# Head norms of memory queries and band queries taken as the scale of the softmax exponential

## The chip, the cores and the metric

The kernel runs on one core of one Trainium2 chip. Its time is the device time of one execution in microseconds (us); three runs of the kernel before gave 1013.49, 1013.75 and 1013.94 us, so the median is 1013.75 us. The engines go by the names of the profile: PE is TensorE (matrix multiply), PEld its weight load, DVE is VectorE, ACT is ScalarE, POOL is GpSimd and SP is the engine that starts the weight transfers. PSUM is the memory of eight banks into which TensorE writes; a bank holds 512 floats per partition.

## The reference

A decoder trunk of two layers on 256 tokens of width 1024, with a memory of 256 tokens. Each layer is an FFN, a mixer and an FFN. Layer 0 mixes with an mLSTM (mixer A below), layer 1 with sliding-window attention of 16 heads of width 64 (mixer B). Both mixers also hold four memory heads of width 128. Queries of the memory heads and of the band heads are normalised per head before their scores are formed:

```python
def rms_norm(x, g):
    y = xf * lax.rsqrt(jnp.mean(xf * xf, axis=-1, keepdims=True) + EPS)
    return y * g

# memory heads
q = rms_norm(xq.reshape(bsz, t, M_HEADS, M_HD), q_norm_g)
s = jnp.einsum('bthd,bmhd->bhtm', q, k) * M_HD ** -0.5
p = jax.nn.softmax(s, axis=-1)
# band heads
q = apply_partial_rope(rms_norm(q, q_norm_g), cos, sin) * B_HD ** -0.5
s = jnp.where(valid, jnp.einsum('bqhgd,bkhd->bhgqk', qn, kn), -jnp.inf)
m = jnp.maximum(jnp.max(s, axis=-1, keepdims=True), sink)
p = jnp.exp(s - m)
denom = jnp.sum(p, axis=-1, keepdims=True) + jnp.exp(sink - m)
```

The norm is one number per token and head. Rotation turns pairs of columns of a row and the scores are linear in the row, so this number may be applied to the row or, later, to the scores.

## The kernel before

Weights are read from memory in tiles of 128 x 1024 and split into a high part (ScalarE, line 213, `wh`) and a low part (VectorE, line 214, `wl`), and each projection product is made of three matmuls (lines 227 to 229, `mm3`). Projections are made in groups of 256 columns: one group fills one PSUM bank with 16 triples, which is 48 matmuls, and the code yields after every four triples, which is 12 matmuls.

The order of TensorE and of SP is the order in which the program emits. Around the main line of groups a class `Weave` keeps a clock of its own, `wv.now`, which each emitted matmul advances by a fixed amount (0.328 for a triple, 0.107 for a transpose, and so on). Side chains are spawned with a delay from the table `LAT`; at each yield of the main line the chains whose time has come are emitted. The order on VectorE, ScalarE and GpSimd is made by the scheduler of the compiler from its own cost model, and each engine then works strictly in that order.

A memory group (two heads, `cross_spawn`, line 595) goes like this. Its bank of raw rows is normalised by `head_norm` (line 395): a square on ScalarE, a sum per head on VectorE (L401), a scale and EPS on VectorE (L404), the power -1/2 on GpSimd (L406), a scale on VectorE (L408), and a multiply of the whole bank into an SBUF tile (L410), after which the bank is free. After a delay `cross` TensorE transposes that tile (L238), ScalarE copies the result out with the gain (`gqk`), and after `cross_s` and `cross_m` the two heads' scores are formed (L233, `bank<-kT,u`). Each head then takes the negated row maximum on VectorE (L618) and the exponential on ScalarE with that maximum as its bias, normalises (L622, L623), transposes the weights, copies them out (L630) and multiplies by the values (L233, `bank<-t,vM`).

A band group (256 columns, four heads of one kind, in mixer B at the end of the file) is normalised in the same way, rotated by `rope` (L884 to L887) in the SBUF tile, and after a delay `query` transposed and copied out with the gain (`gcut`). Each of its two chunks then runs `head`: mask matmuls (L947) and scores (L952) into two banks, four row maxima (L956, L957), the minimum with the sink (L959) and its difference (L960), four exponentials with the maximum as bias, a sum and reciprocal (L968, L969), four multiplies (L973), transposes (L238), copies (L981) and the product with the values (L988).

In mixer B the order of the groups is: keys and values together with the first memory group, the second memory group, four band groups, then the output projection, which keeps four of the eight PSUM banks for itself. In mixer A the two memory groups are followed by the groups of the mLSTM. The keys of the memory and of the band also go through `head_norm`.

Of the kernel before, what the change touches and what calls it, by code (L numbers as in the profile page):

```python
# [32 lines left out]
def constants():  # L33
# [16 lines left out]

LAT = dict(pieces=1, norm=8.5, mnorm=3.5, x0=17.0, mkeys=7.2, cross=9.5, cross_s=1.5,
           cross_m=3.7, cross_p=8.7, cross_o=3.0, gates=20.0, scores=2.2, scores_m=8.4, num=6.9, num_r=7.5,
           keys=5.5, keys_d=7.2, query=9.0, head=1.5, head_m=2.5, head_p=9.3, head_o=4.0)


WARM = 18
# [40 lines left out]
def tile_trunk(ctx: ExitStack, tc: tile.TileContext, a, out):  # L99
# [292 lines left out]
        nc.vector.tensor_scalar_mul(c[:, 2:4], rc, hd ** -0.5 if scaled else 1.0)  # L392
        return c

    def head_norm(dst, src, n, hsc):

        hd = src.shape[2] // n
        sq, v, u = tmp(), col(), col()
        sqv = sq[:, :, :n * hd]
        act(sqv, src, AF.Square)  # L400
        nc.vector.tensor_reduce(out=v[:, 0:2 * n].rearrange("p (h m) -> p h m", h=2),  # L401
                                in_=sqv.rearrange("p h (m d) -> p h m d", m=n), axis=AX.X, op=ALU.add)
        for h in range(2):
            nc.vector.tensor_scalar(u[:, n * h:n * h + n], v[:, n * h:n * h + n], hsc[:, h:h + 1], EPS,  # L404
                                    op0=ALU.mult, op1=ALU.add)
        nc.gpsimd.tensor_tensor(out=u[:, 8:8 + 2 * n], in0=u[:, 0:2 * n], in1=mhalf[:, 0:2 * n], op=ALU.pow)  # L406
        for h in range(2):
            nc.vector.tensor_scalar(v[:, 8 + n * h:8 + n * h + n], u[:, 8 + n * h:8 + n * h + n],  # L408
                                    hsc[:, 2 + h:3 + h], None, op0=ALU.mult)
        tt(out=dst.rearrange("p h (m d) -> p h m d", m=n), in0=src.rearrange("p h (m d) -> p h m d", m=n),  # L410
           in1=v[:, 8:8 + 2 * n].rearrange("p (h m) -> p h m", h=2).unsqueeze(3).to_broadcast([P, 2, n, hd]),
           op=ALU.mult)

    def turn(rows):
# [179 lines left out]

    def cross_spawn(gr, gi, layer, hsc, ys):
        qn = unit(F32)
        head_norm(qn, gr.ps, 2, hsc)
        cell = []

        def queries():  # L600
# [9 lines left out]
        def head(m):  # L610
            hd, qT = gi * 2 + m, cell[0]
            hi, lo = ys.tiles(4 + gi)
            s = mo()
            for h in range(2):
                mmf(s[:, h * T:(h + 1) * T], qT[:, m, h * P:(h + 1) * P], kT[gi][:, m], T)
            sv = halves(s)
            c = col()
            nc.vector.tensor_reduce(out=c[:, 2:4], in_=sv, axis=AX.X, op=ALU.max, negate=True)  # L618
            p = unit(F32)
            for h in range(2):  # L620
                act(p[:, h], sv[:, h], AF.Exp, bias=c[:, 2 + h:3 + h], accum_out=c[:, 4 + h:5 + h])
            nc.vector.reciprocal(c[:, 6:8], c[:, 4:6])  # L622
            tt(out=p, in0=p, in1=c[:, 6:8].unsqueeze(2).to_broadcast([P, 2, T]), op=ALU.mult)  # L623
            yield LAT['cross_p']
            tps = mo()
            for mc in range(2):
                for h in range(2):
                    transpose(tps[:, mc * T + h * P:mc * T + (h + 1) * P], p[:, h, mc * P:(mc + 1) * P])
            pT = tmp()
            nc.scalar.copy(pT, halves(tps))  # L630
# [259 lines left out]
    def mixer_b(x, nxt):  # L890
# [34 lines left out]
        def v22(x4):  # L925
            return x4.rearrange("p (h e) -> p h e", h=2)

        def queries(gi, qn):
            ps = turn(qn)
            qr = unit(F32)  # L930
            act(qr, ps, AF.Copy, scale=gcut[:, 0:1])
            for m in range(2):
                wv.spawn(head(2 * gi + m, qr), LAT['head'] + LAT['head_m'] * m)
            return
            yield

        def head(ch, qr):
# [17 lines left out]
            for e, s in enumerate(sc):  # L955
                nc.vector.tensor_reduce(out=c[:, e:e + 1], in_=s[:, :P], axis=AX.X, op=ALU.max, negate=True)  # L956
                nc.vector.tensor_reduce(out=c[:, 2 + e:3 + e], in_=s[:, P:384], axis=AX.X, op=ALU.max, negate=True)  # L957
            snk = nsink[:, 2 * ch:2 * ch + 2].unsqueeze(1).to_broadcast([P, 2, 2])
            tt(out=v22(c[:, 8:12]), in0=v22(c[:, 0:4]), in1=snk, op=ALU.min)  # L959
# [94 lines left out]
```

## Time and profile before

| | |
|---|---|
| median of three runs | 1013.75 us (1013.49 to 1013.94) |
| profiled execution | span 1011.9 us from the first to the last instruction; its time outside the span is not listed |
| mean granted TensorE clock | 0.997 |
| busy PE, DVE, ACT, POOL | 996.4, 673.3, 524.0, 28.5 us |

The profile page gives busy times, the chain of work that ended last, and groups of instructions by line. A row of a group reads: line, engine, operation, destination<-source, shape, count, then busy us, mean ns of one, and idle us of the engine before them with what ended it. A row of the timeline reads: start and duration in us, engine, line, operation, count, and in brackets the idle time before it with its releaser. A wait row reads: engine, operand and line that waited, what released it, then us in total, times, longest. A row of a window reads: start and end, length, then busy time and count for PE, PEld, DVE, ACT and POOL, the granted TensorE clock, the DMA share and GB/s. Names ending in q are an engine's instruction queue. Line 134 is a helper through which all activations of ScalarE go, and lines 227 to 229 and 233 are helpers for matmuls.

### The profile page before, as it was taken

The page shows a single profiled execution, that of the slowest core. Times are in us where ns is not written, and L with a number is a line of the kernel's source. Part 1 is how long each engine was busy: PE and PEld are TensorE (multiplying, and loading weights), DVE is VectorE, ACT ScalarE, POOL GpSimd, SP SyncE. Part 2 cuts the span into 40 slices and gives each one's busy share as a digit, 9 for nine tenths or more (in the row PEclk, how much of TensorE's full clock was granted, in tenths as well). Part 3 has the DMA queues.
Part 4 walks back from the last instruction along what each step waited for, and adds up shares of the span by engine and source line. Part 5 has one row for each costly group of instructions (what it writes and reads, how often), then busy time and mean ns, then how long its engine had stood idle before and what let it go on. Part 6 is the DMA issues. An engine that isn't in the chain of part 4 may idle for free.

```text
span 1011.9 us, 20587 instructions
## 1 busy us (share of the span) xinstructions
PE 996.4 (98%) x8560; PEld 978.2 (97%) x8560; DVE 673.3 (67%) x1116; ACT 524.0 (52%) x771; POOL 28.5 (3%) x27
## 2 busy tenths in 40 slices
PE   8899999999999999999999999999999999999998
PEld 7899999999999999999999999999987899999998
DVE  6876665668756786666568666656787768666551
ACT  7755444456566564454445444544557665454440
POOL 1100000000100000000000000000121000000000
PEclk9999999999999999999999999999999999999999
DMA  9676666667644566665666666566632247665650
GB/s 310 209 247 189 193 190 180 190 187 204 184 131 138 178 191 199 193 191 178 192 206 201 200 189 192 178 194 199 189 115 81 87 137 222 199 190 183 189 171 22
DMA packets 173205, 182.71 MB, mean 181 GB/s; under 512 B 7124, under 2 KB 168328, under 8 KB 173112
## 3 DMA queue, kind: packets, MB, share of 16 engines
q1 hardware_dynamic: 171872, 179.60, 58.3%
q10 hardware_dynamic: 1016, 1.58, 0.5%
q8 instruction: 67, 1.10, 0.5%
q0 software_dynamic: 224, 0.22, 0.2%
q14 instruction: 26, 0.21, 0.1%
HBM read 180.32 MB, written 1.05 MB: 179 GB/s over the span
## 4 chain that ended last, share of the span: by engine, by line
PE 92%; DVE 4%; ACT 1%; POOL 1%; DMA 1%; issue 0%; SPq 0%; POOLq 0%; ACTq 0%; DVEq 0%
PE bank L227 29%; PE bank L228 29%; PE bank L229 29%; PE bank L233 2%; DVE wl L214 1%; PE bank L238 1%; POOL col L406 1%; ACT u L134 1%; DMA wr<-in_mem_w_kv_dram 1%; PE bank L988 1%; DVE col L401 0%; DVE u L410 0%; DVE u L973 0%; DVE col L957 0%; ACT wh L213 0%
## 5 line engine op out<-in xcount | busy, mean ns | idle before, releaser
L214 DVE TENSOR_TENSOR wl<-wr,wh 128x1024 fp32r<-128x1024 f32 (+1 forms) x347 | 414.7, 1196 | 267.0 <-ACT wh L213 266.2
L213 ACT CAST wh<-wr 128x1024 fp32r<-128x1024 f32 (+1 forms) x347 | 356.9, 1031 | 391.8 <-PE bank L228 367.4
L227 PE MATMUL bank<-xh,wh 128*128 128x256 f32 x1544 | 427.8, 277 | 0.0
L228 PE MATMUL bank<-xl,wh 128*128 128x256 f32 x1544 | 426.4, 276 | 0.0
L229 PE MATMUL bank<-xh,wl 128*128 128x256 f32 x1544 | 426.4, 276 | 0.0
L227 PEld LDWEIGHTS bank<-xh,wh 128*128 128x128 f32 x1544 | 290.0, 188 | 0.1
L228 PEld LDWEIGHTS bank<-xl,wh 128*128 128x128 f32 x1544 | 289.8, 188 | 0.1
L229 PEld LDWEIGHTS bank<-xh,wl 128*128 128x128 f32 x1544 | 289.8, 188 | 0.0
L227 PE MATMUL bank<-u,wh 128*128 128x256 f32 x896 | 249.3, 278 | 0.0
L228 PE MATMUL bank<-u,wh 128*128 128x256 f32 x896 | 247.6, 276 | 0.0
L229 PE MATMUL bank<-u,wl 128*128 128x256 f32 x896 | 247.6, 276 | 0.0
L227 PEld LDWEIGHTS bank<-u,wh 128*128 128x128 f32 x896 | 168.2, 188 | 1.9 <-issue 1.7
L228 PEld LDWEIGHTS bank<-u,wh 128*128 128x128 f32 x896 | 168.3, 188 | 0.1
L229 PEld LDWEIGHTS bank<-u,wl 128*128 128x128 f32 x896 | 168.3, 188 | 0.0
L227 PE MATMUL bank<-wh,xh 128*128 128x256 f32 x208 | 60.3, 290 | 0.0
L228 PE MATMUL bank<-wl,xh 128*128 128x256 f32 x208 | 58.7, 282 | 0.0
L229 PE MATMUL bank<-wh,xl 128*128 128x256 f32 x208 | 58.5, 281 | 0.0
L503 DVE TENSOR_TENSOR t<-bank,rb 128x256 f32<-128x256 f32 x88 | 36.3, 420 | 6.7 <-PE bank L229 6.7
L227 PEld LDWEIGHTS bank<-wh,xh 128*128 128x128 f32 x208 | 39.8, 191 | 0.5 <-issue 0.3
L228 PEld LDWEIGHTS bank<-wl,xh 128*128 128x128 f32 x208 | 39.8, 191 | 0.1
L229 PEld LDWEIGHTS bank<-wh,xl 128*128 128x128 f32 x208 | 39.8, 191 | 0.0
L506 DVE TENSOR_TENSOR t<-t,bank 128x256 f32<-128x256 f32 x88 | 32.7, 413 | 0.0
(182 smaller groups left out, 671.0 us busy)
## 6 DMA issues: line engine op xcount, KB each, us to landing
wr<-in_ffn_w_in_dram SPq DMA_DIRECT2D x176, 512.0 KB, 4.3
wr<-in_ffn_w_out_dram SPq DMA_DIRECT2D x80, 512.0 KB, 3.7
wr<-in_a_w_in_dram SPq DMA_DIRECT2D x28, 512.0 KB, 3.7
wr<-in_b_w_in_dram SPq DMA_DIRECT2D x14, 512.0 KB, 4.6
wr<-in_a_w_out_dram SPq DMA_DIRECT2D x12, 512.0 KB, 3.4
wr<-in_b_w_out_dram SPq DMA_DIRECT2D x12, 512.0 KB, 3.4
wr<-in_ffn_w_out_dram SPq DMA_DIRECT2D x16, 256.0 KB, 2.9
wr<-in_mem_w_kv_dram SPq DMA_DIRECT2D x7, 512.0 KB, 7.8
```

Source lines behind the costliest of these rows:

```text
L134: ins = nc.scalar.activation(*args, **kw)
L213: last[0] = nc.scalar.copy(hi[:, i * n:(i + 1) * n], src[:, i * n:(i + 1) * n])
L214: tt(out=lo[:, i * n:(i + 1) * n], in0=src[:, i * n:(i + 1) * n], in1=hi[:, i * n:(i + 1) * n].bitcast(F32), op=ALU.subtract)
L227: nc.tensor.matmul(ps, wh, xh, start=start, stop=False, skip_group_check=True)
L228: nc.tensor.matmul(ps, wh, xl, start=False, stop=False, skip_group_check=True)
L229: nc.tensor.matmul(ps, wl, xh, start=False, stop=stop, skip_group_check=True)
L233: nc.tensor.matmul(ps, lhsT, rhs, start=start, stop=stop, skip_group_check=True)
L238: nc.tensor.transpose(ps, src, ident[:k, :k])
L406: nc.gpsimd.tensor_tensor(out=u[:, 8:8 + 2 * n], in0=u[:, 0:2 * n], in1=mhalf[:, 0:2 * n], op=ALU.pow)
L503: tt(out=t[:, m], in0=ps[m][:, :T], in1=x.rb, op=ALU.mult)
L506: tt(out=t[:, m], in0=t[:, m], in1=ps[m][:, T:], op=ALU.mult)
L988: nc.tensor.matmul(o[es[e], cs], vr[:, i, js], pTs[e][:, src], start=i == 0, stop=i == 1, skip_group_check=True)
```

## The change

`head_norm` is cut in two. The new `head_factor` makes only the factor per row and head and returns it; `head_norm` calls it and multiplies, and still serves the keys. For memory groups and band groups the bank is now copied raw by ScalarE into the SBUF tile, and the factor is made beside it. Transposes, rotation and scores take the raw rows. In each head the negated maximum of the raw scores is multiplied by the factor on VectorE, and the exponential takes the factor as its scale per partition. Two delays of the emitting clock are changed: `cross` from 9.5 to 5.0 and `query` from 9.0 to 6.5.

```diff
-LAT = dict(... cross=9.5, ... query=9.0, ...)
+LAT = dict(... cross=5.0, ... query=6.5, ...)
...
-    def head_norm(dst, src, n, hsc):
+    def head_factor(src, n, hsc):
         hd = src.shape[2] // n
         sq, v, u = tmp(), col(), col()
...
         for h in range(2):
             nc.vector.tensor_scalar(v[:, 8 + n * h:8 + n * h + n], u[:, 8 + n * h:8 + n * h + n],
                                     hsc[:, 2 + h:3 + h], None, op0=ALU.mult)
+        return v[:, 8:8 + 2 * n].rearrange("p (h m) -> p h m", h=2)
+
+    def head_norm(dst, src, n, hsc):
+        f = head_factor(src, n, hsc)
+        hd = src.shape[2] // n
         tt(out=dst.rearrange("p h (m d) -> p h m d", m=n), in0=src.rearrange("p h (m d) -> p h m d", m=n),
-           in1=v[:, 8:8 + 2 * n].rearrange("p (h m) -> p h m", h=2).unsqueeze(3).to_broadcast([P, 2, n, hd]),
+           in1=f.unsqueeze(3).to_broadcast([P, 2, n, hd]),
            op=ALU.mult)
...
     def cross_spawn(gr, gi, layer, hsc, ys):
         qn = unit(F32)
-        head_norm(qn, gr.ps, 2, hsc)
+        nc.scalar.copy(qn, gr.ps)
+        f = head_factor(gr.ps, 2, hsc)
...
-            nc.vector.tensor_reduce(out=c[:, 2:4], in_=sv, axis=AX.X, op=ALU.max, negate=True)
+            nc.vector.tensor_reduce(out=c[:, 0:2], in_=sv, axis=AX.X, op=ALU.max, negate=True)
+            tt(out=c[:, 2:4], in0=c[:, 0:2], in1=f[:, :, m], op=ALU.mult)
             p = unit(F32)
             for h in range(2):
-                act(p[:, h], sv[:, h], AF.Exp, bias=c[:, 2 + h:3 + h], accum_out=c[:, 4 + h:5 + h])
+                act(p[:, h], sv[:, h], AF.Exp, scale=f[:, h, m:m + 1], bias=c[:, 2 + h:3 + h],
+                    accum_out=c[:, 4 + h:5 + h])
...
         def head(ch, qr, f):
...
+            tt(out=v22(c[:, 0:4]), in0=v22(c[:, 0:4]), in1=f, op=ALU.mult)
             snk = nsink[:, 2 * ch:2 * ch + 2].unsqueeze(1).to_broadcast([P, 2, 2])
...
-                    act(p[e][:, cs], sc[e][:, cs], AF.Exp, bias=c[:, 8 + i:9 + i],
+                    act(p[e][:, cs], sc[e][:, cs], AF.Exp, scale=f[:, h, e:e + 1], bias=c[:, 8 + i:9 + i],
                         accum_out=d[:, 4 + i:5 + i])
...
             qn = unit(F32)
-            head_norm(qn, gr.ps, 4, hsq)
+            nc.scalar.copy(qn, gr.ps)
+            f = head_factor(gr.ps, 4, hsq)
             rope(qn, 4, 0)
-            wv.spawn(queries(gi, qn), LAT['query'])
+            wv.spawn(queries(gi, qn, f), LAT['query'])
```

More of the change, by code (lines that the diff above doesn't have):

```diff
@@ L49 @@
 G_MEM, G_F1, G_MIX, G_F2, G_XQ, G_XK, G_AH, G_BQ, G_BK, G_END = 0, 8, 24, 40, 56, 58, 60, 68, 69, 70
-LAT = dict(pieces=1, norm=8.5, mnorm=3.5, x0=17.0, mkeys=7.2, cross=9.5, cross_s=1.5,
+LAT = dict(pieces=1, norm=8.5, mnorm=3.5, x0=17.0, mkeys=7.2, cross=5.0, cross_s=1.5,
            cross_m=3.7, cross_p=8.7, cross_o=3.0, gates=20.0, scores=2.2, scores_m=8.4, num=6.9, num_r=7.5,
-           keys=5.5, keys_d=7.2, query=9.0, head=1.5, head_m=2.5, head_p=9.3, head_o=4.0)
+           keys=5.5, keys_d=7.2, query=6.5, head=1.5, head_m=2.5, head_p=9.3, head_o=4.0)
 WARM = 18
@@ L926, in v22, with queries @@
             return x4.rearrange("p (h e) -> p h e", h=2)
-        def queries(gi, qn):
+        def queries(gi, qn, f):
             ps = turn(qn)
@@ L932, in queries, with head @@
             for m in range(2):
-                wv.spawn(head(2 * gi + m, qr), LAT['head'] + LAT['head_m'] * m)
+                wv.spawn(head(2 * gi + m, qr, f[:, :, 2 * m:2 * m + 2]), LAT['head'] + LAT['head_m'] * m)
             return
             yield
-        def head(ch, qr):
+        def head(ch, qr, f):
             while wv.now < st.get("at", 1e9):
```

## The prediction

> **What bounds the kernel now.** I read the page first, for the span, the busy times and the chain that ended last.
>
> ```profile
> span 1011.9 us, 20587 instructions
> ...
> PE 996.4 (98%) x8560; PEld 978.2 (97%) x8560; DVE 673.3 (67%) x1116; ACT 524.0 (52%) x771; POOL 28.5 (3%) x27
> ...
> PE 92%; DVE 4%; ACT 1%; POOL 1%; DMA 1%; issue 0%; SPq 0%; POOLq 0%; ACTq 0%; DVEq 0%
> ```
>
> TensorE sets the time. The change removes and adds no matmul, so it can move the end only through the time in which TensorE stands still or runs slowly. The span is 1.85 us below the median of 1013.75 us; I sum changes of the span and apply them to the median. Next I asked for busy times by stage. 230 to 363 us holds the memory-matrix mixer, mixer A; 720 to 838 us holds the band mixer, mixer B. Columns: window, length, PE, PEld, DVE, ACT, POOL, clock.
>
> ```profile
> 230.00:363.00 133.00, 133.00 (x1104) 131.00 (x1103) 98.70 (x213) 79.89 (x140) 7.05 (x6) 1.00 0.54 164
> ...
> 720.00:838.00 118.00, 113.29 (x918) 102.37 (x917) 88.31 (x240) 73.19 (x178) 13.60 (x8) 0.99 0.38 117
> ```
>
> In mixer A TensorE is never idle. Only mixer B has something to win: 118.00 - 113.29 = 4.71 us of idle and a clock of 0.99. The waits of TensorE (engine, line, releaser: us, times, longest) name nearly all of it, 4.64 us:
>
> ```profile
> PE bank L233 <- ACT u L134: 2.4, 1, 2.4
> ...
> PE bank L952 <- ACT u L134: 0.9, 1, 0.9
> PE bank L947 <- DVE u L410: 0.8, 1, 0.8
> PE bank L988 <- ACT u L134: 0.4, 1, 0.4
> ...
> PE bank L947 <- ACT t L981: 0.2, 1, 0.2
> ```
>
> The timeline shows how the first comes about:
>
> ```profile
> 737.42 1.03 PE L233 MATMUL bank<-kT,u 128*128 128x256 f32 x4
> ...
> 739.65 0.60 PE L238 MATMUL bank<-con,u 128*128 128x128 f32 x4
> ...
> 739.76 2.48 POOL L406 TENSOR_TENSOR col<-col,mhalf 128x8 f32<-128x8 f32 x1 [3.46 <-DVE col L404]
> ...
> 742.25 0.28 PE L229 MATMUL bank<-wh,xl 128*128 128x256 f32 x1
> ...
> 742.27 0.36 DVE L408 TENSOR_SCALAR col<-col,qsc 128x4 f32<-128x4 f32 x2 [1.53 <-POOL col L406]
> ...
> 742.54 0.69 DVE L618 TENSOR_REDUCE col<-bank 128x2 f32<-128x512 f32 x1
> ...
> 743.26 0.47 ACT L134 ACTIVATE u<-bank,col 128x256 f32<-128x256 f32 x1 [5.46 <-DVE col L618]
> ...
> 744.17 0.69 ACT L134 ACTIVATE u<-bank,gqk 128x512 f32<-128x512 f32 x1
> ...
> 744.91 1.13 PE L233 MATMUL bank<-kT,u 128*128 128x256 f32 x4 [2.38 <-ACT u L134]
> ```
>
> The first memory scores ran at 737.42. Their maximum (L618) is queued on VectorE behind L408, the head norm of band group 0, which waits for the power on GpSimd. The exponential on ScalarE waits 5.46 us for that maximum, and behind it stands the copy (gqk) of the second memory group's transposes, which TensorE had made at 739.65. TensorE waits 2.38 us for that copy. Then the clock falls (window, length, PE; the clock is the number after POOL), and the same happens after the large waits at the start:
>
> ```profile
> 745.90:749.40 3.50, 3.50 (x18) 3.50 (x17) 2.98 (x7) 2.60 (x10) 0.00 (x0) 0.51 0.37 101
> ...
> 26.50:32.50 6.00, 1.92 (x14) 1.51 (x13) 4.48 (x16) 4.65 (x7) 2.06 (x2) 1.00 0.00 2
> 32.50:36.00 3.50, 3.50 (x19) 3.50 (x18) 3.33 (x6) 1.71 (x3) 1.22 (x1) 0.51 0.57 165
> ```
>
> Its price: the same 24 projection matmuls take 750.25 - 745.69 = 4.56 us there and 737.42 - 734.51 = 2.91 us at full clock, so 1.65 us.
>
> ```profile
> 734.51 0.36 PE L227 MATMUL bank<-wh,xh 128*128 128x256 f32 x1
> ...
> 745.69 0.51 PE L227 MATMUL bank<-wh,xh 128*128 128x256 f32 x1
> ...
> 750.25 0.27 PE L238 MATMUL bank<-con,u 128*128 128x128 f32 x1
> ```
>
> In all, mixer B loses 4.64 + 1.65 = 6.29 us. The change can gain no more than that.
>
> **The change part by part.** *Removed:* the multiply L410 for two memory groups in A and six query groups in B. *Added:* one ScalarE copy per group, one small VectorE multiply per head (4 memory heads per mixer, 8 band chunks), and a scale read per partition in every exponential. Prices from groups of mixer B:
>
> ```profile
> L410 DVE TENSOR_TENSOR u<-bank,col 128x512 f32<-128x512 f32 x6 | 4.1, 690 | 0.3
> ...
> L630 ACT COPY t<-bank 128x512 f32<-128x512 f32 x4 | 2.4, 604 | 0.9 <-PE bank L238 0.9
> ...
> L134 ACT ACTIVATE u<-bank,gqk 128x512 f32<-128x512 f32 x2 | 1.4, 688 | 0.8 <-PE bank L238 0.8
> ...
> L959 DVE TENSOR_TENSOR col<-col,nsink 128x4 f32<-128x4 f32 x8 | 1.3, 160 | 0.2
> ...
> L134 ACT ACTIVATE u<-bank,col 128x256 f32<-128x256 f32 x24 | 11.5, 479 | 7.8 <-DVE col L618 7.8
> ...
> L134 ACT ACTIVATE u<-bank,col 128x128 f32<-128x128 f32 x16 | 6.0, 376 | 9.7 <-DVE col L959 9.7
> ```
>
> VectorE in B: minus 4.1, plus 12 x 0.160 = 1.9, net -2.2 of 88.3 us. ScalarE in B: six copies of 0.604 = 3.6; the scale costs 688 - 604 = 84 ns on a full tile, and on 24 + 16 exponentials 3.4 us; 73.2 becomes 80.2 of 118 us. In A: -1.4 + 0.6 us on VectorE, +1.2 + 0.7 us on ScalarE. Both engines stay under TensorE, so this load costs nothing as a sum. It counts only where TensorE waits for a chain: a band head's exponentials become 4 x 0.084 + 0.16 = 0.5 us longer, a memory head's 0.33 us. The bound from below is 0 (hidden), from above about 0.5 us at each place where TensorE already waits for such a chain.
>
> *Moved:* the raw rows need no sum of squares, no power and no L408. The delays fall to 5.0 (memory queries) and 6.5 (band queries). TensorE's order follows a host clock whose increments stand in the code (0.328 per three projection matmuls, 0.107 per transpose), so both orders can be written down by hand; the one of before agrees with the trace. Call X0, X1 the memory groups, Q0 to Q3 the band groups, H their heads, "4" a quarter of a group (12 matmuls). Before: X1 whole, Q0 4, key turn, Q0 8, X0 turn, Q0 4, Q1 4, X0.0 scores, Q1 4, X1 turn, X0.1 scores, Q1 4, X1.0 scores. After: X1 whole, X0 turn, key turn, Q0 4, X0.0 scores, Q0 8, X0.1 scores, X1 turn, Q0 4, Q1 4, X1.0 scores. No DMA and no weight load changes place, so SP's order stays; GpSimd keeps its powers.
>
> Is the work ready in time? X0's turn comes 12 matmuls before the place of the old key turn (730.89); at 2.91 / 24 = 0.12 us each that is 729.4, where it was 734.15. Its raw copy comes at the latest behind the value copies, in the place of the square at 727.81, and so ends by 728.4. The keys' rows end at 729.94, for a turn at 729.8 (four transposes take 734.51 - 734.15 = 0.36 us) in place of 730.89: 0 to 0.2 us of new wait, I take 0.1. X0.0's scores follow at 731.6; the copy of X0's turn starts behind at most one raw copy and ends near 731.1.
>
> ```profile
> 727.81 0.60 ACT L134 ACTIVATE t<-bank 128x512 f32<-128x512 f32 x1
> ...
> 729.46 0.48 DVE L916 COPY u<-t 128x256 f32<-128x256 f32 x2
> ...
> 730.89 0.60 PE L238 MATMUL bank<-con,u 128*128 128x128 f32 x4
> ...
> 734.15 0.60 PE L238 MATMUL bank<-con,u 128*128 128x128 f32 x4
> ```
>
> The new wait is that of the exponentials for the factor, through the multiply of the maximum. X0's factor existed before the old turn at 734.15, at the latest at 733.5 (a multiply of 0.69 stood between); its exponential then starts by 734.3, and behind it on ScalarE stand weight casts and the copy of X1's turn, which TensorE wants only two thirds of a group later. Q0's factor has the time from its group's end, near 738, to H0's scores, some ten microseconds.
>
> X0.0's maximum is due near 732.4, long before Q0's power starts (Q0 ends near 738), and 24 matmuls stand between X1's turn and X1.0's scores in place of 12 and a memory score. The place of the 2.38 us wait is dissolved: I take the full 2.38 and, with no long gap, the 1.65 of the clock.
>
> The Trainium skill, "TensorE: Matmul & The Clock Gate", section "HAM oscillation — how this bites in real kernels", lets the clock fall only after gaps of more than about 3.4 us. By that rule a 2.4 us gap would not explain the slow window and its 1.65 us need not return (estimate by it: a gain of 3.1 us before losses). The trace shows the fall right behind a single wait of 2.38 us, and once more behind a stretch with 4.1 of 6 us idle, so I go by the trace.
>
> The 0.8 us wait at L947 is for the bank of Q3, held until L410:
>
> ```profile
> 783.67 0.69 DVE L410 TENSOR_TENSOR u<-bank,col 128x512 f32<-128x512 f32 x1
> ...
> 784.42 0.32 PE L947 MATMUL bank<-maskb,identb 128*128 128x384 bf16 x1 [0.75 <-DVE u L410]
> ```
>
> After the change the bank comes free when copy and square (2 x 0.6 us) are done, without sums and power: gain 0.75.
>
> The 0.9 us wait is that of the band scores for the copy of Q1's turn, which stood behind the exponentials of two heads:
>
> ```profile
> 758.98 0.60 PE L238 MATMUL bank<-con,u 128*128 128x128 f32 x4
> ...
> 759.12 0.37 ACT L134 ACTIVATE u<-bank,col 128x128 f32<-128x128 f32 x1 [1.53 <-DVE col L959]
> ...
> 762.74 0.74 ACT L134 ACTIVATE u<-bank,gcut 128x512 f32<-128x512 f32 x1
> ```
>
> The scores were due 0.9 us before that copy's end at 763.5, 3.6 us after the turn. By the host clock the distance from Q1's turn to H2's scores falls from 3.4 to 2.7, or some 2.9 us; but H1's exponentials now lie further ahead of the turn. Bounds: -0.9 (the wait goes) and +1.4 (the copy as late as now, 4.5 us, and 8 x 0.084 later, against 2.9, less the 0.9 that stands). I take 0, the wait as it is, near the middle. In the output projection four banks are bound to it, and H6, H7 and the transposes of H5 now follow each other closer: a bank wait there, bounded by 0 and the time for which a head's four exponentials hold it (2 x 0.479 + 2 x 0.376 and the scale, some 2 us); I take 0.5, nearest to the 0.2 and 0.4 that stand there now.
>
> In mixer A X0's turn moves behind the whole of X1's group, which is 5.8 us of matmuls against a copy of 0.6 us; I cost it at 0, and what hides the added work there is that cover.
>
> Sum: -2.38 - 1.65 - 0.75 + 0.1 + 0.5 = -4.2 us; 1013.75 - 4.2 = 1009.6 us.
>
> **The rivals.** (1) *All waits go:* the band-score and bank waits vanish too: -6.29, 1007.5 us. For it: less VectorE work, banks free earlier. Against it: ScalarE gets 7 us more. Chance 0.14. (2) *The clock does not come back:* the half-speed window had another cause than the wait and falls anyway: -4.2 + 1.65, 1011.2 us. For it: 2.38 us is less than the window's own 3.5. Against it: both windows stand behind idle stretches. Chance 0.09. (It is what the rule of the Trainium skill's "TensorE: Matmul & The Clock Gate", cited above, would give.) (3) *The stall moves to the band queries:* the copy of Q1's turn stays behind two heads' exponentials (759.12 to 762.74), with a cover of only 2.9 us: a wait of 0.9 + 1.4 = 2.3 us, enough for a slow window again, 1.4 + 1.65 = 3.1 us back; 1012.7 us. Chance 0.12. (4) *Slower:* the same mechanism at Q1 and at Q2, whose distance shrinks by the host clock from 3.4 to 2.7 as well: 3.1 + 2.3 + 1.65 = 7.1 us back, 1016.7 us. It decides once two such copies end over 2.3 us late; one alone isn't enough. For it: VectorE's and ScalarE's order is planned by a model that already misplaced L408. Against it: the heads before Q2 are spread wider. Chance 0.15. That the scores come no earlier because the raw copy is itself late is within (3).
>
> **How the numbers follow.** My forecast has 0.50. A measurement of this kernel tells about 0.2% (2 us) from no change. Faster: the forecast, (1), (2) and a small part of (3), 0.74; same: the rest of (3), 0.11; slower: (4), 0.15. The range reaches from a little below all waits gone, 1007.0, past (3) to 1014.0, and leaves out (4) and little else. The likeliest case alone: 1008.5 to 1010.8.
>
> **What would show it.** Right: no wait of over 1 us at L233 behind ScalarE; clock 1.00 through 720 to 838; X0's turn near 729.4; no wait of the mask matmuls (L947 now) for a query group's bank; mixer A still without idle TensorE. Wrong: a wait of over 2.4 us at the band scores with a half-clock window behind it, or mixer B's idle again over 4 us; idle TensorE in mixer A.

## The result and the profile after

The changed kernel takes 1025.71 us (1024.69 to 1028.57, 4 runs) against 1013.85 us (1013.49 to 1014.39) for the kernel before: a ratio of 1.0115, with a 95% interval of 1.0103 to 1.0127. It is slower by 1.15%, where I had forecast 1009.6 us and a range up to 1014.0. The profiled run took 1026.1 us.

The page of the changed kernel: span, busy time of the engines, share of each engine in the chain that ended last.

```profile
span 1024.3 us, 20611 instructions
...
PE 1000.6 (98%) x8560; PEld 980.7 (96%) x8560; DVE 670.7 (65%) x1124; ACT 532.1 (52%) x779; POOL 24.5 (2%) x27
...
PE 88%; DVE 5%; ACT 3%; POOL 1%; issue 1%; DMA 1%; SPq 0%; ACTq 0%; POOLq 0%
```

The load moved as worked out: VectorE 2.6 us less, ScalarE 8.1 us more, the same 8560 matmuls. But in the chain VectorE has 5% instead of 4 and ScalarE 3% instead of 1. The span grew by 12.4 us. I measure each mixer from the matmul of its own norm (L308) to the next norm's: mixer A went from 133.05 to 137.07 us, mixer B from 115.53 to 124.12, together 12.6 us; the rest of the program gives back 0.2.

Windows of the changed kernel over mixer A, mixer B and three short stretches (columns as in the prediction; the number after POOL is the granted clock):

```profile
229.40:366.50 137.10, 134.59 (x1105) 132.41 (x1104) 98.41 (x214) 81.54 (x142) 6.32 (x6) 0.99 0.52 160
725.90:850.10 124.20, 114.01 (x897) 101.60 (x897) 84.98 (x244) 78.28 (x182) 10.27 (x8) 0.97 0.34 107
270.60:274.00 3.40, 3.40 (x17) 3.40 (x16) 1.77 (x3) 1.79 (x5) 0.00 (x0) 0.50 0.30 66
772.30:775.70 3.40, 3.40 (x17) 2.80 (x14) 2.95 (x10) 1.23 (x3) 0.00 (x0) 0.50 0.02 5
789.40:792.80 3.40, 3.32 (x16) 2.67 (x17) 2.45 (x11) 1.59 (x5) 1.20 (x1) 0.50 0.14 45
```

Mixer A, never idle before, now has 2.51 us of idle TensorE and a stretch at half clock. Mixer B has 10.2 us of idle instead of 4.7, and two stretches at half clock instead of one. With 1.65 us for each such stretch (the price worked out in the prediction) that is 2.5 + 1.65 in A and 5.5 + 1.65 in B, 11.3 of the 12.6 us. Another 1.4 us of mixer B is longer busy time of TensorE that I did not trace to one place.

The waits of TensorE in the changed kernel (line, releaser: us in total, times, longest):

```profile
PE bank L233 <- ACT u L134: 4.2, 2, 2.5
PE bank L961 <- ACT u L134: 3.9, 3, 2.7
...
PE bank L956 <- ACT u L134: 2.0, 3, 1.1
```

These are scores and masks that wait for ScalarE's copy of a turn (the transposed queries) or for a bank that exponentials hold. The chain behind the first of them, in mixer A (timeline: start, duration, engine and line; in brackets how long the engine had waited and for whom):

```profile
258.64 1.02 PE L233 MATMUL bank<-kT,u 128*128 128x256 f32 x4
...
260.32 1.01 POOL L406 TENSOR_TENSOR col<-col,mhalf 128x4 f32<-128x4 f32 x1 [1.46 <-DVE col L404]
261.36 0.36 DVE L408 TENSOR_SCALAR col<-col,qsc 128x2 f32<-128x2 f32 x2 [1.12 <-POOL col L406]
261.63 0.69 DVE L625 TENSOR_REDUCE col<-bank 128x2 f32<-128x512 f32 x1
262.23 1.22 DVE L214 TENSOR_TENSOR wl<-wr,wh 128x1024 fp32r<-128x1024 f32 x1
262.33 1.03 PE L233 MATMUL bank<-kT,u 128*128 128x256 f32 x4
...
263.20 0.60 PE L238 MATMUL bank<-con,u 128*128 128x128 f32 x4
263.36 0.15 DVE L626 TENSOR_TENSOR col<-col,col 128x2 f32<-128x2 f32 x1
...
264.84 0.17 DVE L631 RECIPROCAL col<-col 128x2 f32<-128x2 f32 x1 [1.33 <-ACT u L134]
...
265.65 0.68 DVE L625 TENSOR_REDUCE col<-bank 128x2 f32<-128x512 f32 x1
266.25 1.22 DVE L214 TENSOR_TENSOR wl<-wr,wh 128x1024 fp32r<-128x1024 f32 x1
...
267.38 0.15 DVE L626 TENSOR_TENSOR col<-col,col 128x2 f32<-128x2 f32 x1
...
267.63 0.56 ACT L134 ACTIVATE u<-bank,col,col 128x256 f32<-128x256 f32 x1 [1.88 <-DVE col L626]
...
268.73 0.68 ACT L134 ACTIVATE u<-bank,gqk 128x512 f32<-128x512 f32 x1
...
269.47 1.13 PE L233 MATMUL bank<-kT,u 128*128 128x256 f32 x4 [2.51 <-ACT u L134]
```

X0.0's scores end at 259.66, but their maximum (L625) starts only at 261.63. VectorE runs its instructions in order, and ahead of the maximum stands L408 of the *other* group's factor, which waits for the power on GpSimd. Then comes the second delay: between each maximum (L625) and its multiply (L626) stands a weight cast (L214, 1.22 us), so that the exponential, which needs the multiply's result, starts over a microsecond later. The delay of the first head is passed on to the second: X0.1's scores end at 263.36, but its maximum starts 2.29 us later, because the normalisation of X0.0 (L631) stands ahead of it and waits for X0.0's late exponentials. The copy of X1's turn (gqk) stands behind X0.1's exponentials on ScalarE; TensorE had made that turn at 263.20 and waits 2.51 us for the copy.

The memory place of mixer B is the one whose wait I had called dissolved. Timeline:

```profile
735.55 1.03 PE L233 MATMUL bank<-kT,u 128*128 128x256 f32 x4
...
736.84 1.22 DVE L214 TENSOR_TENSOR wl<-wr,wh 128x1024 fp32r<-128x1024 f32 x1
737.98 0.67 DVE L401 TENSOR_REDUCE col<-t 128x4 f32<-128x512 f32 x1
...
738.95 0.69 DVE L625 TENSOR_REDUCE col<-bank 128x2 f32<-128x512 f32 x1
...
740.23 0.36 DVE L408 TENSOR_SCALAR col<-col,qsc 128x2 f32<-128x2 f32 x2 [0.59 <-POOL col L406]
740.50 0.15 DVE L626 TENSOR_TENSOR col<-col,col 128x2 f32<-128x2 f32 x1
...
745.27 1.13 PE L233 MATMUL bank<-kT,u 128*128 128x256 f32 x4 [1.74 <-ACT u L134]
```

The scores end at 736.58; a weight cast and the other group's sum of squares (L401) put the maximum off by 2.4 us, and L408 puts the multiply off once more. At the band queries the same two things come together, with the longest wait of all:

```profile
760.34 0.93 PE L961 MATMUL bank<-u,u 64*128 64x128 f32 x8
...
765.35 0.36 DVE L408 TENSOR_SCALAR col<-col,qsc 128x4 f32<-128x4 f32 x2 [1.55 <-POOL col L406]
...
766.05 0.63 PE L238 MATMUL bank<-con,u 128*128 128x128 f32 x4 [0.76 <-DVE u L896]
766.16 0.28 DVE L965 TENSOR_REDUCE col<-bank 128x1 f32<-128x128 f32 x1
...
767.55 0.15 DVE L967 TENSOR_TENSOR col<-col,col 128x4 f32<-128x4 f32 x1
767.62 1.21 DVE L214 TENSOR_TENSOR wl<-wr,wh 128x1024 fp32r<-128x1024 f32 x1
...
768.94 0.46 ACT L134 ACTIVATE u<-bank,col,col 128x128 f32<-128x128 f32 x1 [4.60 <-DVE col L969]
...
771.00 0.69 ACT L134 ACTIVATE u<-bank,gcut 128x512 f32<-128x512 f32 x1
...
771.75 1.14 PE L961 MATMUL bank<-u,u 64*128 64x128 f32 x8 [2.67 <-ACT u L134]
```

H1's scores end at 761.27. Their maxima (L965) stand behind L408 of Q1's factor and start at 766.16; a cast stands between the multiply (L967) and the next step; ScalarE waits 4.60 us, and the copy of Q1's turn, behind H1's exponentials, is 2.67 us late for H2's scores. Half clock follows at 772.3.

The same comes again at Q2, with two casts in the chain of H3 (VectorE and the waits of TensorE, in the timeline):

```profile
782.06 0.36 DVE L408 TENSOR_SCALAR col<-col,qsc 128x4 f32<-128x4 f32 x2 [1.56 <-POOL col L406]
...
783.59 1.21 DVE L214 TENSOR_TENSOR wl<-wr,wh 128x1024 fp32r<-128x1024 f32 x1
...
784.80 1.22 DVE L214 TENSOR_TENSOR wl<-wr,wh 128x1024 fp32r<-128x1024 f32 x1
...
787.27 0.32 PE L956 MATMUL bank<-maskb,identb 128*128 128x384 bf16 x1 [0.24 <-ACT u L134]
788.26 0.32 PE L956 MATMUL bank<-maskb,identb 128*128 128x384 bf16 x1 [0.66 <-ACT u L134]
```

Two masks wait for exponentials, and H4's scores at 789.48 wait 0.90 us for the copy of Q2's turn; half clock follows at 789.4. With the smaller waits behind it, up to the output projection of the last heads, TensorE waits 4.4 us here, where the kernel before had 1.35 us (0.75, 0.4 and 0.2). So B's idle grew by 2.8 us around Q1 (0.9 became 2.67, 0.76 and 0.31) and by 3.0 us from Q2 on, and shrank by 0.3 us at the memory groups (2.38 became 1.74 and 0.35).

### The profile page after: what moved, and what is told of

It is laid out like the page before. It is cut to its first block, busy times and chain, and to the rows that moved or that the text cites. A ratio compares the mean times of both kernels' runs of the same rounds, so it can differ in the third digit from the quotient of the medians.

```text
span 1024.3 us, 20611 instructions
## 1 busy us (share of the span) xinstructions
PE 1000.6 (98%) x8560; PEld 980.7 (96%) x8560; DVE 670.7 (65%) x1124; ACT 532.1 (52%) x779; POOL 24.5 (2%) x27
## 3 DMA queue, kind: packets, MB, share of 16 engines
HBM read 180.32 MB, written 1.05 MB: 177 GB/s over the span
## 4 chain that ended last, share of the span: by engine, by line
PE 88%; DVE 5%; ACT 3%; POOL 1%; issue 1%; DMA 1%; SPq 0%; ACTq 0%; POOLq 0%
PE bank L228 28%; PE bank L227 28%; PE bank L229 28%; ACT u L134 2%; DVE wl L214 2%; PE bank L233 1%; POOL col L406 1%; PE bank L238 1%; DMA wr<-in_mem_w_kv_dram 1%; ACT wh L213 1%; DVE col L401 0%; PE bank L961 0%; DVE col L966 0%; PE bank L998 0%; DVE u L983 0%
## 5 line engine op out<-in xcount | busy, mean ns | idle before, releaser
L214 DVE TENSOR_TENSOR wl<-wr,wh 128x1024 fp32r<-128x1024 f32 (+1 forms) x347 | 414.8, 1197 | 272.8 <-ACT wh L213 271.8
L227 PE MATMUL bank<-xh,wh 128*128 128x256 f32 x1544 | 428.4, 277 | 0.0
L227 PEld LDWEIGHTS bank<-xh,wh 128*128 128x128 f32 x1544 | 290.5, 188 | 0.1
L227 PE MATMUL bank<-u,wh 128*128 128x256 f32 x896 | 249.4, 278 | 0.3 <-ACT t L991 0.3
L227 PEld LDWEIGHTS bank<-u,wh 128*128 128x128 f32 x896 | 168.3, 188 | 1.8 <-issue 1.2
L227 PE MATMUL bank<-wh,xh 128*128 128x256 f32 x208 | 60.4, 291 | 0.0
L227 PEld LDWEIGHTS bank<-wh,xh 128*128 128x128 f32 x208 | 39.6, 190 | 1.5 <-issue 1.4
L134 ACT ACTIVATE u<-bank,col,col 128x256 f32<-128x256 f32 (+1 forms) x48 | 24.8, 526 | 25.0 <-DVE col L626 13.7
```

Of the source, the lines that this page charges most:

```text
L134: ins = nc.scalar.activation(*args, **kw)
L214: tt(out=lo[:, i * n:(i + 1) * n], in0=src[:, i * n:(i + 1) * n], in1=hi[:, i * n:(i + 1) * n].bitcast(F32), op=ALU.subtract)
L227: nc.tensor.matmul(ps, wh, xh, start=start, stop=False, skip_group_check=True)
```

## The experiments

Two theories stood at the start. O: the new order alone costs the time, since turns and scores stand closer than ScalarE's copies allow. C: the chain to the exponential costs it, through L408 or the new multiply on VectorE. Ratios are to the kernel before, run beside each of them (medians 1013.85 us for the change, 1014.33 to 1014.72 us for the others). Stage lengths are measured as above; those of the kernel before are 133.05 and 115.53 us. e5 and e12 leave the norm of the queries out of the result; all others compute the whole function.

| run | us | ratio (95%) | A | B |
|---|---|---|---|---|
| change | 1025.71 | 1.0115 (1.0103–1.0127) | 137.07 | 124.12 |
| e1_old_delays | 1014.34 | 1.000 (0.9991–1.001) | 132.99 | 115.42 |
| e2_order_only | 1023.16 | 1.0079 (1.0062–1.0096) | 134.97 | 122.07 |
| e3_memory_only | 1023.6 | 1.0087 (1.0063–1.0111) | 137.13 | 122.06 |
| e4_band_only | 1019.1 | 1.0038 (1.0025–1.0052) | 132.99 | 119.25 |
| e5_no_multiply | 1020.84 | 1.0062 (1.0045–1.0079) | 132.99 | 121.51 |
| e6_factor_gpsimd | 1015.55 | 1.0017 (1.0008–1.0026) | 133.84 | 116.53 |
| e7_distance | 1018.31 | 1.0044 (1.0029–1.0059) | 133.05 | 119.91 |
| e8_old_delays_gpsimd | 1011.66 | 0.9969 (0.996–0.9979) | 132.99 | 111.35 |
| e9_before_gpsimd | 1015.23 | 1.0009 (1.0–1.0019) | 133.05 | 115.83 |
| e10_gpsimd_head3 | 1011.33 | 0.9961 (0.9947–0.9975) | 132.99 | 110.96 |
| e11_both_gpsimd | 1020.11 | 1.005 (1.0035–1.0065) | 133.69 | 119.20 |
| e12_no_multiply_gpsimd | 1012.08 | 0.9972 (0.9963–0.9982) | 132.94 | 112.62 |

The sizes were hard to foresee: e3 came out above every range that had been stated for it, e6 below, and e2, e7, e8 and e12 between two ranges (e8 and e12 by less than 1 us).

### The arithmetic without the order, and the order without the arithmetic

```diff
 # e1_old_delays, against the change
-LAT = dict(... cross=5.0, ... query=6.5, ...)
+LAT = dict(... cross=9.5, ... query=9.0, ...)
```

> The change with the delays of before (9.5 and 9.0): the new arithmetic alone, the order on TensorE as before. Theory O (the order does it): no loss is left, 1010 to 1015 us, mixer A without idle TensorE. Theory C (the head's chain does it: the added multiply behind the maximum, with weight casts let in between, holds the exponential, and the copies of the next transposes stand behind it): most of the 12 us stays, 1020 us or more, and mixer A still shows a wait at the memory scores of over 1.5 us.

1014.34 us, no difference from the kernel before. So the loss needs the new delays, as theory O had it; theory C alone had 1020 us or more. The raw rows alone bring nothing: the wait that I wanted gone stands almost unchanged. The waits of TensorE in e1:

```profile
PE bank L233 <- ACT u L134: 2.3, 1, 2.3
PE bank L961 <- ACT u L134: 1.6, 1, 1.6
```

```diff
 # e2_order_only, against the kernel before
-LAT = dict(... cross=9.5, ... query=9.0, ...)
+LAT = dict(... cross=5.0, ... query=6.5, ...)
```

> The kernel before with the new delays (5.0 and 6.5) and the old arithmetic: the order alone. Theory O: at least as slow as the changed kernel, 1025 us or more. Theory C: the transposes now also wait for rows that are not yet normalised, by up to 734.15 - 729.4 = 4.8 us less 1 us of slack in B, so 1016 to 1022 us, with the waits at the transposes (line 238) behind the multiply of the bank and not at the scores.

1023.16 us, but for another reason than in the changed kernel: here the turns wait for the normalised rows (waits for L410: 5.7 us at the turns and 2.8 us at L227), which the change does away with. So this loss does not separate O from C.

### The two places, one at a time

```diff
 # e3_memory_only, against the change: band queries as before
-LAT = dict(... query=6.5, ...)
+LAT = dict(... query=9.0, ...)
-            nc.scalar.copy(qn, gr.ps)
-            f = head_factor(gr.ps, 4, hsq)
+            head_norm(qn, gr.ps, 4, hsq)
...
-            tt(out=v22(c[:, 0:4]), in0=v22(c[:, 0:4]), in1=f, op=ALU.mult)
...
-                    act(p[e][:, cs], sc[e][:, cs], AF.Exp, scale=f[:, h, e:e + 1], bias=c[:, 8 + i:9 + i],
+                    act(p[e][:, cs], sc[e][:, cs], AF.Exp, bias=c[:, 8 + i:9 + i],
```

> The change for the memory queries alone; band queries as before with their delay of 9.0. It has all of the 4.2 us that mixer A lost. Theory C: 4.2 us in A and some 2 us in B, 1018 to 1022 us. Theory O: A's 4.2 us and, with the band order back, a B no slower than before: 1013 to 1018 us.

```diff
 # e4_band_only, against the change: memory queries as before
-LAT = dict(... cross=5.0, ...)
+LAT = dict(... cross=9.5, ...)
-        nc.scalar.copy(qn, gr.ps)
-        f = head_factor(gr.ps, 2, hsc)
+        head_norm(qn, gr.ps, 2, hsc)
...
-            tt(out=c[:, 2:4], in0=c[:, 0:2], in1=f[:, :, m], op=ALU.mult)
...
-                act(p[:, h], sv[:, h], AF.Exp, scale=f[:, h, m:m + 1], bias=c[:, 2 + h:3 + h],
+                act(p[:, h], sv[:, h], AF.Exp, bias=c[:, 2 + h:3 + h],
```

> The change for the band queries alone; memory queries as before with their delay of 9.5. Mixer A has no idle TensorE and gains 0. Theory C: B keeps the 2.4 us wait of before at the memory scores and adds waits of the band scores for the copy of their transposes: 1017 to 1022 us. Theory O: 1012 to 1016 us.

The memory half alone gives 1023.6 us, more than either theory had allowed: mixer A loses its whole 4 us, and B loses 6.5 us, partly at band scores (a wait of 3.1 us at L961) that this kernel does not edit. The band half alone gives 1019.1 us, all in B, with a wait of 2.9 us at the memory scores, which it does not edit either. As ratios the two parts add up to about the whole (0.87% and 0.38% against 1.15%, within the intervals). By stage they add up in A (4.1 and -0.1 against 4.0 us) but not in B (6.5 and 3.7 against 8.6): each edit moves VectorE's whole order, and the wait shows where that order has put something ahead of a maximum. In e3 the first of the two heads ahead of the 3.1 us wait has its maximum 2.45 us after its scores, behind L408, the multiply of the rows, the rotation and a cast; in e4 the memory head has its own 4.64 us after, right behind Q0's L408.

### The multiply and the wait for the power, one at a time and together

```diff
 # e5_no_multiply, against the change (the same at the band heads)
-            nc.vector.tensor_reduce(out=c[:, 0:2], in_=sv, axis=AX.X, op=ALU.max, negate=True)
-            tt(out=c[:, 2:4], in0=c[:, 0:2], in1=f[:, :, m], op=ALU.mult)
+            nc.vector.tensor_reduce(out=c[:, 2:4], in_=sv, axis=AX.X, op=ALU.max, negate=True)
...
-                act(p[:, h], sv[:, h], AF.Exp, scale=f[:, h, m:m + 1], bias=c[:, 2 + h:3 + h],
+                act(p[:, h], sv[:, h], AF.Exp, scale=ones[:, 0:1], bias=c[:, 2 + h:3 + h],
```

> The changed kernel without the multiply of the maximum: the exponentials take the raw maximum as bias and a column of ones as scale, so their cost is the same and the norm of the queries is left out of the result; the factor itself is still made. Theory C (casts let in between maximum and multiply): the 1.2 us casts at the two first memory heads of mixer A no longer lie in the chain, so A loses 1.5 to 2.5 us less than its 4.1 and the whole is 1017 to 1021 us. Theory O (the new order, with the copies behind the exponentials): 1023 us or more.

1020.84 us. Taking out sixteen multiplies of 0.16 us brings 4.9 us: with them goes the place between a maximum and its exponential into which, in the timelines above, casts were put. Mixer A is back at 132.99 us, although X0.0's maximum still starts 1.97 us after its scores there; mixer B still loses 6.0 us. The edit also frees the exponentials from the factor itself, and no run separates the two. In the changed kernel X0's own factor was ready (L408 ended at 259.26 in A and at 736.93 in B) before X0.0's maximum started (261.63 and 738.95), so there it held up nothing.

```diff
 # e6_factor_gpsimd, against the change: L408's step follows the power on GpSimd
-        for h in range(2):
-            nc.vector.tensor_scalar(v[:, 8 + n * h:8 + n * h + n], u[:, 8 + n * h:8 + n * h + n],
-                                    hsc[:, 2 + h:3 + h], None, op0=ALU.mult)
-        return v[:, 8:8 + 2 * n].rearrange("p (h m) -> p h m", h=2)
+        f = v[:, 8:8 + 2 * n].rearrange("p (h m) -> p h m", h=2)
+        nc.gpsimd.tensor_tensor(out=f, in0=u[:, 8:8 + 2 * n].rearrange("p (h m) -> p h m", h=2),
+                                in1=hsc[:, 2:4].unsqueeze(2).to_broadcast([P, 2, n]), op=ALU.mult)
+        return f
```

> The changed kernel with the factor's last scale (line 408) made on GpSimd behind the power, so that nothing on VectorE but the multiply itself waits for the power. Theory P (the power's wait holds the next head's maximum on VectorE): A loses 2 to 4 us less, B 2 us or more less, 1017 to 1021 us. Theory O or C: 1023 us or more.

1015.55 us: with the multiply kept, 10.2 of the 11.9 us are gone. The timeline of e6 in mixer A, to be read beside that of the change:

```profile
259.80 1.22 DVE L214 TENSOR_TENSOR wl<-wr,wh 128x1024 fp32r<-128x1024 f32 x1
259.98 1.94 POOL L406 TENSOR_TENSOR col<-col,mhalf 128x4 f32<-128x4 f32 x1 [220.69 <-DVE col L404]
...
261.57 1.02 PE L233 MATMUL bank<-kT,u 128*128 128x256 f32 x4
...
262.46 1.01 POOL L406 TENSOR_TENSOR col<-col,mhalf 128x4 f32<-128x4 f32 x1 [0.27 <-DVE col L404]
262.63 0.69 DVE L625 TENSOR_REDUCE col<-bank 128x2 f32<-128x512 f32 x1 [0.24 <-PE bank L233]
263.24 1.22 DVE L214 TENSOR_TENSOR wl<-wr,wh 128x1024 fp32r<-128x1024 f32 x1
...
264.37 0.15 DVE L626 TENSOR_TENSOR col<-col,col 128x2 f32<-128x2 f32 x1
```

The scores end at 262.59 and the maximum starts at 262.63, although GpSimd's power for the other group is still running; in the changed kernel it started 1.97 us after its scores. The cast between maximum and multiply (263.24) is still there. The longest wait left in e6, at the band scores, brings one stretch at half clock (768.1):

```profile
PE bank L961 <- ACT u L134: 1.7, 1, 1.7
```

```diff
 # e12_no_multiply_gpsimd: the edits of e5 and of e6 together
```

> The changed kernel with its new delays, the last scale on GpSimd and no multiply of the maximum (raw maximum as bias, a column of ones as scale: the norm of the queries is left out of the result). With the multiply, GpSimd gave 1015.6 us, without it and the scale on VectorE 1020.8 us. If the power's wait and the multiply with its casts are all that makes the new delays lose: 1008 to 1012 us, as fast as the delays of before with GpSimd. If the new order loses by itself (copies behind exponentials, banks of the output projection): 1013 to 1016 us.

1012.08 us, faster than the kernel before by 0.28% (0.18 to 0.37). Windows of e12 over mixers A and B:

```profile
230.90:363.90 133.00, 133.00 (x1105) 130.88 (x1104) 97.56 (x206) 81.65 (x142) 7.30 (x8) 1.00 0.55 165
723.40:836.00 112.60, 109.96 (x896) 98.92 (x895) 81.43 (x218) 77.83 (x182) 14.22 (x15) 1.00 0.37 118
```

TensorE idles 2.6 us in B, and the clock stays at 1.00. The four runs at the new delays make a square: 1.0115 with both, 1.0062 without the multiply, 1.0017 with the power's result kept off VectorE, 0.9972 without either. Without the two the whole loss is gone, so neither theory holds alone: the new arithmetic costs nothing in the old order (e1), and the new order costs nothing without these two steps on VectorE (e12). The loss is what order and steps make together in VectorE's queue; the wait has the larger share (10.2 us alone, against 4.9 for the multiply). In mixer A taking away either is enough or nearly so (132.99 and 133.84 us), since the 2.51 us take both a late maximum and two casts; in mixer B the wait counts most. (The 1.97 us by which the maximum was late and a cast of some 1.05 us in each of two heads are more than the wait.) Each of these kernels has an order of its own on VectorE and ScalarE, so the runs price an edit together with the new order it brings, and not one instruction in a fixed order.

### More distance, and the multiply on GpSimd too

```diff
 # e7_distance, against the change
-LAT = dict(... cross_s=1.5, ... head=1.5, ...)
+LAT = dict(... cross_s=4.5, ... head=4.0, ...)
```

> The changed kernel with the scores further behind the transposes: cross_s 4.5 for 1.5 and head 4.0 for 1.5 (X1's turn then comes before the scores of X0's second head). Theory O: the waits of the scores for the copies (lines 233 and 961) fall from 8.1 to under 3 us and with them most half-clock windows; 1012 to 1018 us. Theory C: the chain is as long as before and meets the weights' transposes instead; 1020 us or more.

1018.31 us: with the scores moved away from their turn, the long waits for the copies of turns are gone, and mixer A is full again. Mixer B keeps half of its loss in another place: the value products now wait for copies of weights' transposes and for exponentials (at L233 2.2 us in three waits, at L998 2.2 us and, in two waits, 1.7). Distance treats the wait; it does not shorten the chain that causes it.

```diff
 # e11_both_gpsimd, against e6
-            tt(out=c[:, 2:4], in0=c[:, 0:2], in1=f[:, :, m], op=ALU.mult)
+            nc.gpsimd.tensor_tensor(out=c[:, 2:4], in0=c[:, 0:2], in1=f[:, :, m], op=ALU.mult)
...
-            tt(out=v22(c[:, 0:4]), in0=v22(c[:, 0:4]), in1=f, op=ALU.mult)
+            nc.gpsimd.tensor_tensor(out=v22(c[:, 0:4]), in0=v22(c[:, 0:4]), in1=f, op=ALU.mult)
```

> The changed kernel, its new delays, with the factor's last scale and the multiply of the maximum on GpSimd, so that neither the power nor a cast on VectorE stands between the maximum and its multiply. Theory C on top of P: the rest of what the new delays lose goes too, 1011 to 1014 us. If the queue of GpSimd (powers of 1.0 to 2.9 us) takes the place of VectorE's: 1016 to 1022 us.

1020.11 us, worse than e6 by 4.6 us. The multiplies now stand in GpSimd's queue, behind the powers, and the round trip lies in every head's chain: waits at the masks (L956, 1.9 us) and value products (L233, 1.8 us) come back. Three of the sixteen multiplies took 1.05 to 1.13 us beside a weight cast, against 0.19 to 0.20 us for twelve of the others, so the slower multiplies have a part in it too; no run tells the two apart. Taking a step off VectorE helped where the step itself waits for GpSimd, not where it feeds from VectorE and back.

### Is there a gain, and from what

```diff
 # e8_old_delays_gpsimd: the edit of e6, and the delays of the kernel before
-LAT = dict(... cross=5.0, ... query=6.5, ...)
+LAT = dict(... cross=9.5, ... query=9.0, ...)
```

> The change with the delays of before (9.5 and 9.0) and the factor's last scale on GpSimd. Theory P: the 2.3 us wait at the memory scores of mixer B and its half-clock window go, 1008 to 1011 us, faster than the kernel before. Theories O and C: 1013 to 1015 us.

```diff
 # e9_before_gpsimd: the kernel before, with only L408's step on GpSimd (in head_norm)
-        for h in range(2):
-            nc.vector.tensor_scalar(v[:, 8 + n * h:8 + n * h + n], ...
+        nc.gpsimd.tensor_tensor(out=v[:, 8:8 + 2 * n].rearrange("p (h m) -> p h m", h=2), ...
```

> The kernel before with nothing but the factor's last scale on GpSimd (control for the gain of the old delays with GpSimd). There the multiply of the bank (line 410) still stands on VectorE and waits for the factor in the same place. Theory P with raw rows needed: no gain, 1012.5 to 1015.5 us, and the 2.4 us wait at the memory scores of mixer B stays. If the gain came from the move alone: 1010 to 1012 us.

e8 gives 1011.66 us, faster than the kernel before (0.9969) with the whole function computed; e9 gives 1.0009, no gain, with its wait of 2.6 us at L233 still there. In e8 that wait is gone: X0.0's maximum in B starts 1.07 us after its scores, behind a cast, while Q0's power is still running; in the kernel before it started 4.09 us after them. e1 (raw rows, the wait on VectorE) gave 1.000. So neither the raw rows nor the move to GpSimd brings anything alone; the two together do. In e9 the multiply of the rows itself (L410) still waits on VectorE for GpSimd, 10.5 us in seven waits; with raw rows no instruction of the query groups on VectorE does.

```diff
 # e10_gpsimd_head3, against e8
-LAT = dict(... head=1.5, ...)
+LAT = dict(... head=3.0, ...)
```

> The change with the delays of before, the last scale on GpSimd and the band scores further behind their transposes (head 3.0 for 1.5). What is left in mixer B with the delays of before and GpSimd is one wait of 1.5 us at the band scores of chunk 2 behind the exponentials of chunks 0 and 1. If it goes without another in its place: 1009 to 1011 us; if the later heads meet the four banks of the output projection: 1011 to 1014 us.

1011.33 us, 0.9961 (0.9947 to 0.9975): the best version of this study, ahead of both kernels, and not to be told from e8 by its interval. Mixer B in e10:

```profile
724.50:835.40 110.90, 109.25 (x896) 98.74 (x895) 82.76 (x230) 77.92 (x182) 19.80 (x15) 1.00 0.38 119
```

Of the 4.71 us of idle TensorE before, 1.65 are left, and the clock does not fall in this mixer. GpSimd is busy for 19.8 us instead of 13.6, and none of TensorE's waits there names it. The shorter delays, in contrast, lost in each of the three pairs: 1025.71 against 1014.34 (the change and e1), 1015.55 against 1011.66 (e6 and e8), and e2 against the kernel before (where the cause is the late rows).

## Why the prediction was wrong, by its own steps

**The step that failed first: "X0.0's maximum is due near 732.4, long before Q0's power starts", so "the place of the 2.38 us wait is dissolved".** TensorE's order came out as I had written it by hand: counted from the norm matmul, I had X0's turn at 7.2 us and X0.0's scores at 9.4; they came at 7.3 and 9.6. But I let the maximum run when it was due. It stood in VectorE's queue behind a cast and X1's own sum of squares, at 13.0 us instead of 10.2, and then its multiply behind X1's L408. I had looked for one power only (Q0's) and had asked which is later; each group has one, and with the turns brought forward X1's lay in the way. 1.74 of the 2.38 us stayed. The half-clock stretch behind it did go, as forecast, but by luck: the wait had not gone, it only fell well against the clock's periods (last section). The row that should have warned me was in the prediction itself: the maximum queued behind L408, with ScalarE waiting 5.46 us. I moved the work away from that collision and did not ask what VectorE's queue would hold at the new place. e6 and e8 show the size of this step.

**The term that was mis-sized: "one small VectorE multiply" of 0.160 us, a memory head's chain "0.33 us longer".** The instruction took 0.15 us and an exponential 0.56 instead of 0.47 us, as worked out. But a new dependent step on VectorE is also a new place in its queue, and a cast of 1.22 us came to stand in it in both heads of X0 in mixer A, and in some of the heads in B. The chain grew by 1.2 us a head, not by 0.16. With it gone (e5) the time fell by 4.9 us.

**"In mixer A ... I cost it at 0."** The cover that I named (5.8 us of matmuls over a copy of 0.6 us) was that of X0's turn; it held, and the wait came at X1's turn, which in the new order is what B's X1 turn was in the old: a copy behind another head's exponentials. 2.51 us and a stretch at half clock, 4.0 us that my range had no case for.

**"Bounds: -0.9 ... and +1.4 ... I take 0, the wait as it is."** At Q1 the wait grew from 0.9 to 2.67 us, 1.8 more, past the bound of 1.4. I had taken the copy "as late as now", but H1's maxima were put off by L408 and a cast. Rival (4) named both places (Q1 and Q2), the sign and the mechanism (copies of band turns behind exponentials, a planner that already misplaced L408), with a chance of 0.15 and 1016.7 us. What it lacked is that the same queue also holds up the memory groups, in both mixers.

**"A bank wait there, bounded by 0 and ... some 2 us; I take 0.5".** From Q2 on TensorE waited eight times, 3.0 us longer in all than before, and had a second stretch at half clock, 1.65 us. 1.8 of it are the three waits around Q2's turn, which belong to rival (4) too; the others, up to 1.12 us, are masks, transposes and value products behind the exponentials of the heads ahead. I had bounded one wait and not counted how many heads pass there.

**What was right.** The load: VectorE's and ScalarE's sums did not matter. The bank wait of 0.75 us for L410 went, though masks now wait 2.0 us for exponentials. DMA and weight loads stood still. A stretch at half clock follows a long wait, and its price of 1.65 us fits mixer A, where 4.0 less 2.5 us leaves 1.5. A gain of about the size forecast is there to be had, 4.2 us (0.41%) in the prediction and 0.39% in e10; but it comes from keeping VectorE's queue free and not from the shorter delays, so that the sizes agree is chance.

## What to carry to other kernels

When a change brings work forward, write the order of the in-order engines at the new place as carefully as that of the bounding one: "ready" is when the queue lets an instruction run, and an instruction that waits for another engine holds everything behind it. A small dependent step added between a reduction and its consumer costs what the scheduler puts ahead of it, here 1.2 us for 0.15. Here a step whose only late input came from another engine went to that engine with gain (e6, e8), and a step that became a round trip lost there (e11).

## What the runs showed of the hardware

In the mixers of all these traces TensorE fell to half clock after every single wait of 1.9 us or more (from 1.93 in e11 over 2.38 before, 2.51 and 2.67 in the changed kernel to 3.84 in e2), for 3.41 us except once in e3 (6.83). Near 1.7 us it went both ways: it fell in e6 (1.67 at L961) and did not in the changed kernel (1.74 at 745.27) nor in e4 (1.83); after 1.61 us or less (e1) it did not, except that the stretch at 789.4 in the changed kernel followed waits of 0.24, 0.66 and 0.90 us close together. The Trainium skill, "TensorE: Matmul & The Clock Gate", section "HAM oscillation — how this bites in real kernels", puts the bound at gaps above about 3.4 us; here the measurement differs and decides.

The clock records of the traces show what tells these cases apart. Within a trace the stretches start whole multiples of 3.413 us from each other: in the changed kernel at 270.57, 772.33 and 789.39 (147 and 5 periods), in the kernel before at 32.59 and 745.98 (209 periods). If the mixers of all fourteen traces are cut into these periods and TensorE's idle time is added up in each, half clock followed all 13 periods with more than 1.83 us of idle, none with less than 1.66, and four of the six between. So what counted here was the idle time within one period, at about half of it, and not the length of one wait: of the 1.74 us at 745.27 only 1.49 lay in one period, while the three short waits before 789.4 put 1.72 us into one.

The power on GpSimd (L406, 128x4) took 1.01 us alone (260.32 in the changed kernel) and 1.94 us where a weight cast was already running on VectorE (259.98 in e6, behind the cast at 259.80). The Trainium skill, "SBUF — State Buffer", section "Who interferes with whom", says that VectorE and GpSimd share one pair of ports to SBUF which only one can hold. The trace agrees (the cast reads two SBUF tiles), with about 0.9 us for one power. A power that had started before the cast was not slowed: 1.01 us at 261.60 in e8, with a cast from 261.96 on. Nor was it the long rest before it: at 259.56 in e8 it took 1.03 us after 221.7 us of rest. In the mixers of the changed kernel each of the nine powers had L408 waiting for it on VectorE, 10.6 us in all.
